# Row-wise max-norm of a float32 matrix: partial maxima folded in by VectorE's own last instruction of a row instead of by GpSimd

## The chip, the cores and the metric

The kernel runs on one core of a Trainium2 chip. The metric is device microseconds of one execution; three runs of the kernel before gave 628.87, 628.88 and 628.91 us, median 628.88 us. Times in the profile are counted from the first instruction that the profiler saw.

## The reference

```python
def setup_inputs():
    return {"x": np.random.randn(8192, 8192).astype(np.float32)}

def reference(x):
    return np.linalg.norm(x, ord=np.inf, axis=1)
```

The vector infinity norm of each of 8192 rows is the largest absolute value in the row. Every one of the 268.4 MB of x has to be read once, and the output is 32 KB.

## The kernel before

**Two parts.** The first 8192 - 18*128 = 5888 rows (the big part) are read by 23 loads. A load brings two whole rows to each of the 128 partitions (16384 columns of float32 a partition, 8 MB). The last 2304 rows (the tail) give each partition 18 rows that follow each other in memory, so a partition's tail is one run of 18*8192 = 147456 columns. It is cut into 29 loads without regard to where rows end. I number the loads 0 to 22 (big) and 23 to 51 (tail); load 23 is again 16384 wide, and the widths then fall to 704.

**The planner.** `tail_loads` chooses the widths. It holds two straight lines, `LOAD` (1.1775 ns a column and 73 ns a load) and `REDUCE` (1.0417 ns a column and 60 ns an instruction), and walks back from the end so that each load lands just before VectorE has finished with the one before it. The last piece of the last row is 704 wide, and the last piece of row 16 (768 wide) is loaded just before it, out of order.

**Pieces and rows.** Where a load ends inside a row, the row comes in pieces. In the tail, rows 0, 1, 2 and 4 to 8 are whole. Rows 3 and 9 to 14 have two pieces each, row 15 has three, row 16 five, row 17 seven. A load can hold the end of one row and the beginning of the next; VectorE then runs one instruction for each.

**The ring.** All loads land in one SBUF tensor, `ring`, of 3*16384 columns a partition, with 2048 more behind it (`APART`) for the last load. `Pieces.room` hands out places in order and goes back to column 0 when a load does not fit in what is left. All widths are multiples of 64, so every load begins at a multiple of 64 columns (256 bytes).

**Queues and waits.** All loads are issued by SyncE (L92) in order. A load's landing is counted on one of five semaphores in turn, and load i may be issued only after VectorE's last instruction for load i-5; it also waits for whatever VectorE still has to read in the columns that it overwrites. VectorE runs one `tensor_reduce` (maximum of absolute values, L110) a piece, in order of the loads; the first of a load waits for the load's semaphore. Consecutive instructions overlap a little: an instruction that waits for nothing starts about 0.08 us before the one before it ends.

**Partial maxima.** For rows 3 and 9 to 16 each piece's maximum goes to a small tensor `parts`, and GpSimd takes the maximum of them into `res_tail` (L207), ten instructions in all. Row 17 is done differently: its partial maxima are written to `ring` just behind the place of its last piece (load 51, at column 49152), and the instruction for that piece reads six columns more and takes them in.

**The end.** Two one-element memsets on VectorE (L218) keep the last store's wait apart from the last reduction. ScalarE issues the store of the big part (L221) and of tail rows 0 to 15 (L225). SyncE first waits for GpSimd's result of row 16 (`seen`, L236), then for VectorE's memsets, and issues the store of rows 16 and 17 (L240); the program ends when that has landed and the engines have met at a barrier.

Of the kernel before, what the change touches and what calls it, by code (L numbers as in the profile page):

```python
# [7 lines left out]
P = 128  # L8
R = 2
RING = 3 * 16384  # L10
APART = 2048
# [6 lines left out]
ROWS = 18  # L18
# [7 lines left out]
def tail_loads(n_cols, big):  # L26

    slack = 0.0
    lag = REDUCE[0] * FIRST + REDUCE[1]
    loads = []
    end = ROWS * n_cols

    def take(top, bottom, most):
        nonlocal slack  # L40
        w = 0
        n = 0
        spare = SPARE if loads else 0
        while True:

            n += 1
            start = max(bottom, (top - 1) // n_cols * n_cols - (n - 1) * n_cols)
            fit = int((lag + slack - spare - REDUCE[1] * n) / REDUCE[0])
            w = max(w, min(fit, top - start) // GRAIN * GRAIN)
            if fit <= top - start or start <= bottom:  # L50
                break
        w = max(GRAIN, min(w, most, top - bottom))
        row = (top - w + n_cols - 1) // n_cols * n_cols
        if top - row >= SNAP * w or (w == most and top > row):
            w = top - row
        n = (top - 1) // n_cols - (top - w) // n_cols + 1
        slack += (LOAD[0] - REDUCE[0]) * w + LOAD[1] - REDUCE[1] * n
        loads.append((top - w, w))
        return top - w

    ends = [take(end, end - n_cols, FIRST), take(end - n_cols, end - 2 * n_cols, n_cols)]
    for top, bottom in zip(ends, (end - n_cols, 0)):
        while top > bottom:
            top = take(top, bottom, big)
    return loads[::-1]
# [60 lines left out]
@with_exitstack  # L126
def kernel(
    ctx: ExitStack,
    tc: tile.TileContext,
    x: bass.AP,  # L130
    out: bass.AP,
):
    nc = tc.nc
    f32 = mybir.dt.float32
    n_rows, n_cols = x.shape

    tail = tail_loads(n_cols, R * n_cols)
    split = n_rows - ROWS * P
    n_big = split // (R * P)

    x_big = x[:split].rearrange("(p t r) m -> t p (r m)", p=P, r=R)
    x_tail = x[split:].rearrange("(p r) m -> p (r m)", p=P)

    single = ctx.enter_context(tc.tile_pool(name="single", bufs=1))
    ring = single.tile([P, RING + APART], f32)
    res_big = single.tile([P, n_big, R], f32)
    res_tail = single.tile([P, ROWS], f32)
    idle = single.tile([1, IDLE], f32)  # L150
    pieces = Pieces(tc, ring)

    for t in range(n_big):
        at = pieces.room(R * n_cols)
        pieces.load(at, R * n_cols, x_big[t])
        buf = ring[:, at : at + R * n_cols]
        pieces.reduce([(res_big[:, t, :], buf.rearrange("p (r m) -> p r m", r=R))])


    parts = []  # L160
    for i, (start, w) in enumerate(tail):
        c = 0
        while c < w:
            row = (start + c) // n_cols
            n = min(w - c, (row + 1) * n_cols - start - c)
            parts.append((row, i, c, n))
            c += n
    of_row = [[q for q in parts if q[0] == row] for row in range(ROWS)]

    spots, behind, dst = {}, {}, {}
    at = RING
    for row, own in enumerate(of_row):
        if row == ROWS - 1:
            spots[own[-1][1]] = at
            at += own[-1][3]
            for q in own[:-1]:
                dst[q] = ring[:, at : at + 1]
                at += 1  # L180
            behind[own[-1]] = len(own) - 1
            dst[own[-1]] = res_tail[:, row : row + 1]
        elif len(own) == 1:
            dst[own[0]] = res_tail[:, row : row + 1]
        else:
            some = single.tile([P, len(own)], f32, name=f"parts{row}")
            for k, q in enumerate(own):
                dst[q] = some[:, k : k + 1]
    assert at <= RING + APART and len(behind) == 1
    for i, (start, w) in enumerate(tail):  # L190
        at = spots[i] if i in spots else pieces.room(w)
        pieces.load(at, w, x_tail[:, start : start + w])
        done = pieces.reduce(
            [
                (dst[q], ring[:, at + q[2] : at + q[2] + q[3] + behind.get(q, 0)])
                for q in parts
                if q[1] == i
            ]
        )
        for row in range(ROWS - 1):  # L200
            if len(of_row[row]) > 1 and of_row[row][-1][1] == i:
                best = dst[of_row[row][0]]
                more = [dst[q] for q in of_row[row][1:]]
                while more:
                    two, more = more[:2], more[2:]
                    to = best if more else res_tail[:, row : row + 1]
                    combined = nc.gpsimd.tensor_scalar(  # L207
                        out=to,
                        in0=best,
                        scalar1=two[0],  # L210
                        scalar2=two[1] if len(two) == 2 else None,
                        op0=mybir.AluOpType.max,
                        **(dict(op1=mybir.AluOpType.max) if len(two) == 2 else {}),
                    )
                    tc.add_to_no_dep_group("combined", combined.ins)
    tc.declare_fence(done.ins, group="loads")
    for i in range(IDLE):
        rest = nc.vector.memset(idle[:, i : i + 1], 0.0)  # L218
        tc.keep_in_program_order(rest)

    early = nc.scalar.dma_start(  # L221
        out=out[:split].rearrange("(p q) -> p q", p=P), in_=res_big.rearrange("p t r -> p (t r)")
    )
    out_tail = out[split:].rearrange("(p r) -> p r", p=P)
    middle = nc.scalar.dma_start(  # L225
        out=out_tail[:, : ROWS - 2], in_=res_tail[:, : ROWS - 2]
    )
    for store in (early, middle):
        tc.add_manual_dep(
            store.ins,  # L230
            pieces.last[-3].name,
            mybir.DependencyInfo(mybir.DependencyClass.Sync, mybir.DependencyReason.DATA),
            reason="not beside the last load",
        )

    seen = nc.sync.keepalive_nop([nc.sync.lower_ap(res_tail[:, ROWS - 2 : ROWS - 1])])  # L236
    tc.keep_in_program_order(seen)
    tc.no_tile_sem_insts.add(seen.ins.name)
    tc.add_to_no_dep_group("seen", seen.ins)
    last = nc.sync.dma_start(out=out_tail[:, ROWS - 2 :], in_=res_tail[:, ROWS - 2 :])  # L240
    tc.declare_no_dep(last.ins, group="combined", reason="SyncE has waited for GpSimd")
    tc.declare_fence(last.ins, group="seen")
    for before in (rest, early, middle):
        gone = nc.sync.keepalive_nop([])
        tc.keep_in_program_order(gone)
        tc.add_manual_dep(
            gone.ins,
            before.ins.name,
            mybir.DependencyInfo(mybir.DependencyClass.Sync, mybir.DependencyReason.DATA),
            reason="done before the last store lands",  # L250
        )
# [28 lines left out]
```

## Time and profile before

| | before |
|---|---|
| median of three runs | 628.88 us |
| the profiled execution itself | 628.88 us |
| its span, first to last instruction | 627.1 us |
| outside the span | 1.78 us |
| VectorE busy | 552.1 us, 62 instructions |
| GpSimd busy | 3.2 us, 14 instructions |
| HBM read | 268.44 MB, 428 GB/s over the span |
| VectorE's wait for loads, big part | 69.4 us |
| VectorE's wait for loads, tail | 2.1 + 1.2 us |
| last store issued, span | 624.92 us |

A group line of the page reads: line, engine, operation, what is written from what, shapes, count, busy microseconds, mean nanoseconds of one, idle time of the engine just before, and what ended that idle time. Only gaps over 0.15 us count as idle there. DMA's own work stands in the lines on GB/s and in the time from a load's issue to its landing.

### The profile page before, as it was taken

Reading aid. Unit: us, or ns where it says so; the run is one execution under the profiler, and the core shown is the slowest. Engines: PE = TensorE matmul, PEld = TensorE weight load, DVE = VectorE, ACT = ScalarE, POOL = GpSimd, SP = SyncE. Lnnn points to the kernel's source line nnn. Section 1 sums busy time; section 2 is a strip of 40 time slices with the busy share of each in tenths; the row PEclk is TensorE's granted clock in tenths of the full one; section 3 lists DMA queues with packets and bytes.
Section 4 is the critical chain, followed back from the end, with each engine's and each line's share of the span. In section 5 each row is a group of like instructions: output and inputs, shape, how many; then the busy total and the mean of one; then the engine's idle time right before and its main releaser. Section 6 shows DMA issues by size and latency. Waiting matters only on the chain.

```text
span 627.1 us, 175 instructions
## 1 busy us (share of the span) xinstructions
DVE 552.1 (88%) x62; POOL 3.2 (1%) x14
## 2 busy tenths in 40 slices
DVE  0588988889988889888898888988889999999998
POOL 0000000000000000000000000000000000000000
DMA  9999999999999999999999999999999999999997
GB/s 401 410 460 401 468 401 468 401 468 401 468 401 468 401 468 401 468 401 468 401 464 405 451 418 451 418 439 431 422 437 442 404 435 442 430 422 430 426 422 308
DMA packets 7921, 268.48 MB, mean 428 GB/s; under 512 B 1264, under 2 KB 1264, under 8 KB 2416
## 3 DMA queue, kind: packets, MB, share of 16 engines
q1 hardware_dynamic: 7632, 268.44, 99.3%
q10 hardware_dynamic: 288, 0.03, 0.0%
q14 instruction: 1, 0.01, 0.0%
HBM read 268.44 MB, written 0.03 MB: 428 GB/s over the span
## 4 chain that ended last, share of the span: by engine, by line
DMA 57%; DVE 42%; issue 0%; DVEq 0%; SPq 0%
DMA ring<-in_x_dram 57%; DVE res_big L110 22%; DVE parts L110 12%; DVE res_tail L110 7%; DVE ring L110 1%; DVEq L275 0%; SPq L92 0%; DVE idle L218 0%
## 5 line engine op out<-in xcount | busy, mean ns | idle before, releaser
L110 DVE TENSOR_REDUCE res_big<-ring 128x2 f32<-128x16384 f32 x23 | 396.1, 17220 | 69.4 <-DMA ring<-in_x_dram 69.4
L110 DVE TENSOR_REDUCE parts<-ring 128x1 f32<-128x3136 f32 (+18 forms) x22 | 78.5, 3634 | 1.2 <-DMA ring<-in_x_dram 1.2
L110 DVE TENSOR_REDUCE res_tail<-ring 128x1 f32<-128x8192 f32 (+1 forms) x9 | 69.8, 7811 | 2.1 <-DMA ring<-in_x_dram 2.1
L110 DVE TENSOR_REDUCE ring<-ring 128x1 f32<-128x1600 f32 (+5 forms) x6 | 8.3, 1445 | 0.0
L207 POOL TENSOR_SCALAR res_tail<-parts 128x1 f32<-128x1 f32 x9 | 2.7, 296 | 615.6 <-DVE parts L110 615.6
L207 POOL TENSOR_SCALAR parts<-parts 128x1 f32<-128x1 f32 x1 | 0.4, 353 | 5.6 <-DVE parts L110 5.6
L264 POOL MEMSET const-bfloat16-1.0<- 128x1 bf16 x1 | 0.1, 101 | 0.0
L264 POOL MEMSET const-uint8-127<- 128x1 uint8 x1 | 0.1, 101 | 0.0
L264 POOL MEMSET const-float32-0.0<- 128x1 f32 x1 | 0.1, 99 | 0.2 <-issue 0.2
L264 POOL MEMSET const-float32-1.0<- 128x1 f32 x1 | 0.1, 98 | 0.0
L218 DVE MEMSET idle<- 1x1 f32 x2 | 0.1, 59 | 0.0
## 6 DMA issues: line engine op xcount, KB each, us to landing
ring<-in_x_dram SPq DMA_DIRECT2D x3, 4096.0 KB, 40.5
ring<-in_x_dram SPq DMA_DIRECT2D x1, 7264.0 KB, 31.1
ring<-in_x_dram SPq DMA_DIRECT2D x1, 5024.0 KB, 33.3
ring<-in_x_dram SPq DMA_DIRECT2D x1, 4544.0 KB, 34.6
ring<-in_x_dram SPq DMA_DIRECT2D x1, 4224.0 KB, 40.3
ring<-in_x_dram SPq DMA_DIRECT2D x1, 4032.0 KB, 35.5
ring<-in_x_dram SPq DMA_DIRECT2D x1, 3584.0 KB, 35.4
ring<-in_x_dram SPq DMA_DIRECT2D x2, 1568.0 KB, 18.3
```

What stands on the lines that cost most here:

```text
L110: ins = self.nc.vector.tensor_reduce(out=dst, in_=src, axis=mybir.AxisListType.X, op=mybir.AluOpType.max, apply_absolute_value=True,)
L207: combined = nc.gpsimd.tensor_scalar(out=to, in0=best, scalar1=two[0], scalar2=two[1] if len(two) == 2 else None, op0=mybir.AluOpType.max, ...
L218: rest = nc.vector.memset(idle[:, i : i + 1], 0.0)
L264: nc = _bacc.Bacc("TRN2", target_bir_lowering=False, num_devices=1)
```

## The change

GpSimd takes no part any more. For every tail row that comes in several pieces, the maxima of the pieces before the last are written to the columns of `ring` right in front of the place of the row's last piece, and VectorE's instruction for that last piece starts that many columns earlier. To make the room, `room` is asked for the piece's width plus the number of partial maxima, and the load starts behind them. Row 17's partials move from behind its last piece to the front of it, too. Where a load holds the end of a row and the beginning of the next, the beginning of the next row is now reduced first.

```diff
-    spots, behind, dst = {}, {}, {}
-    at = RING
+    ahead = [0] * len(tail)
+    for own in of_row:
+        assert own[-1][2] == 0 or len(own) == 1
+        ahead[own[-1][1]] += len(own) - 1
+    places = [pieces.room(ahead[i] + w) + ahead[i] for i, (_, w) in enumerate(tail[:-1])]
+    places.append(RING + ahead[-1])
+    dst = {}
     for row, own in enumerate(of_row):
...
+        at = places[own[-1][1]] - (len(own) - 1)
+        for k, q in enumerate(own[:-1]):
+            dst[q] = ring[:, at + k : at + k + 1]
+        dst[own[-1]] = res_tail[:, row : row + 1]
     for i, (start, w) in enumerate(tail):
-        at = spots[i] if i in spots else pieces.room(w)
+        at = places[i]
         pieces.load(at, w, x_tail[:, start : start + w])
...
-                while more:
-                    two, more = more[:2], more[2:]
-                    to = best if more else res_tail[:, row : row + 1]
-                    combined = nc.gpsimd.tensor_scalar(
...
+        mine = sorted((q for q in parts if q[1] == i), key=lambda q: -q[2])
+        pairs = []
+        for q in mine:
+            before = len(of_row[q[0]]) - 1 if q == of_row[q[0]][-1] else 0
+            pairs.append((dst[q], ring[:, at + q[2] - before : at + q[2] + q[3]]))
+        done = pieces.reduce(pairs)
...
-    seen = nc.sync.keepalive_nop([nc.sync.lower_ap(res_tail[:, ROWS - 2 : ROWS - 1])])
-    tc.keep_in_program_order(seen)
...
     last = nc.sync.dma_start(out=out_tail[:, ROWS - 2 :], in_=res_tail[:, ROWS - 2 :])
```

What follows from it for places, worked out from the widths: a load's width plus its partials is no longer a multiple of 64, so loads 25 to 27 and 30 to 51 begin 1 to 6 columns (4 to 24 bytes) past a multiple of 64 columns, load 50 nine columns past it. Load 28 no longer fits behind load 27 (8191 columns are left, 8192 are needed) and goes to column 0, where load 24 lay; load 34 goes back to column 1. VectorE has the same 60 reductions over the same columns.

More of the change, by code (lines that the diff above doesn't have):

```diff
@@ L168 @@
     of_row = [[q for q in parts if q[0] == row] for row in range(ROWS)]
-    spots, behind, dst = {}, {}, {}
-    at = RING
-    for row, own in enumerate(of_row):
[L175 to L188, printed above, removed]
@@ L189 @@
-    assert at <= RING + APART and len(behind) == 1
+    ahead = [0] * len(tail)
[4 more added lines that the diff above has]
+    places.append(RING + ahead[-1])
+    assert places[-1] + tail[-1][1] <= RING + APART
+    dst = {}
+    for row, own in enumerate(of_row):
+        at = places[own[-1][1]] - (len(own) - 1)
+        for k, q in enumerate(own[:-1]):
+            dst[q] = ring[:, at + k : at + k + 1]
+        dst[own[-1]] = res_tail[:, row : row + 1]
@@ L190 @@
     for i, (start, w) in enumerate(tail):
-        at = spots[i] if i in spots else pieces.room(w)
+        at = places[i]
         pieces.load(at, w, x_tail[:, start : start + w])
[L193 to L203, printed above, removed]
-                while more:
-                    two, more = more[:2], more[2:]
-                    to = best if more else res_tail[:, row : row + 1]
[L207 to L215, printed above, removed]
@@ L234 @@
         )
-    seen = nc.sync.keepalive_nop([nc.sync.lower_ap(res_tail[:, ROWS - 2 : ROWS - 1])])
-    tc.keep_in_program_order(seen)
-    tc.no_tile_sem_insts.add(seen.ins.name)
-    tc.add_to_no_dep_group("seen", seen.ins)
     last = nc.sync.dma_start(out=out_tail[:, ROWS - 2 :], in_=res_tail[:, ROWS - 2 :])
-    tc.declare_no_dep(last.ins, group="combined", reason="SyncE has waited for GpSimd")
-    tc.declare_fence(last.ins, group="seen")
     for before in (rest, early, middle):
```

## The prediction

> **What bounds the kernel now.** I read the busy shares and the DMA lines of the page first, then the table of stretches, then the chain of waits, then the last two microseconds instruction by instruction.
>
> ```profile
> span 627.1 us, 175 instructions
> DVE 552.1 (88%) x62; POOL 3.2 (1%) x14
> ...
> HBM read 268.44 MB, written 0.03 MB: 428 GB/s over the span
> ...
> L110 DVE TENSOR_REDUCE res_big<-ring 128x2 f32<-128x16384 f32 x23 | 396.1, 17220 | 69.4 <-DMA ring<-in_x_dram 69.4
> ...
> L207 POOL TENSOR_SCALAR res_tail<-parts 128x1 f32<-128x1 f32 x9 | 2.7, 296 | 615.6 <-DVE parts L110 615.6
> ```
>
> VectorE is 88% busy, but in the big part it waits 69.4 us for loads: there the transfer is the bound. GpSimd's ten combining instructions take 3.1 us in all. The table of stretches (columns: length, VectorE busy and instructions, GpSimd busy, clock, share of the DMA engines, GB/s):
>
> ```profile
> 41.80:467.60 425.80, 378.83 (x22) 0.00 (x0) 1.00 1.00 432
> ...
> 497.00:546.00 49.00, 49.00 (x6) 0.28 (x1) 1.00 1.01 434
> 546.00:594.00 48.00, 48.00 (x12) 1.39 (x5) 1.00 0.99 426
> 594.00:624.00 30.00, 30.00 (x16) 0.99 (x3) 1.00 0.98 404
> ```
>
> From 497 us on both are full: VectorE 49.00 of 49.00, 48.00 of 48.00, 30.00 of 30.00 us, and the DMA engines 0.98 to 1.01. The chain of waits names VectorE for this stretch, but only by a hair. A load's landing is its issue plus its time to landing. By that, load 30 landed at 546.61 and VectorE began it at 546.65; load 37: 594.00 and 594.05; load 46: 618.28 and 618.30; load 51: 623.95 and 624.01. A reduction that really waits for a load starts 0.023 us after the landing (467.596 to 467.619), so the two are within 0.04 us of each other from 546 us to the end. Whatever slows either of them in the tail moves the end; making one faster gains nothing beyond 0.04 us.
>
> ```profile
> 623.15 0.94 DVE L110 TENSOR_REDUCE parts<-ring 128x1 f32<-128x768 f32 x1
> ...
> 624.01 0.89 DVE L110 TENSOR_REDUCE res_tail<-ring 128x1 f32<-128x710 f32 x1
> 624.27 0.36 POOL L207 TENSOR_SCALAR res_tail<-parts 128x1 f32<-128x1 f32 x1 [10.84 <-DVE parts L110]
> 624.84 0.06 DVE L218 MEMSET idle<- 1x1 f32 x2
> 624.92 0.35 SPq L240 DMA_DIRECT2D out_dram<-res_tail  x1
> ```
>
> In these rows (start, length) GpSimd's last instruction ends at 624.63 and VectorE's memsets at 624.90; the last store is issued 0.025 us after the memsets. GpSimd is 0.27 us off the path.
>
> **The change part by part.**
>
> *GpSimd and SyncE's wait for it go: 0.* Ten instructions, 3.1 us, all beside VectorE and DMA. SyncE's wait for GpSimd ended at 624.67, before VectorE's end at 624.90, which stays and releases the store. ScalarE's store of rows 0 to 15 waited for a GpSimd instruction that ended at 607.5, and is still held behind the big store to 623.68.
>
> *Longer reads: +0.014 us.* 19 partial maxima are read in front of pieces, six of which row 17 read before; 13 more elements at 1.05 ns (8676 ns for 8192 less 4275 ns for 3968, over 4224 columns, is 1.04).
>
> *Order inside a load: 0.* Where a load holds an end and a beginning, the same two instructions run in the other order, with the same sum. The load's columns come free at the same end.
>
> *VectorE's waits on itself.* Twelve reductions more than before now wait for an earlier reduction: to read partials that it wrote, or to write partials where something was read before. Counting back in the order of the instructions, the awaited one is two or more places back in all but one case, so it ended before the waiting instruction could start. The last instruction of before has such a wait, two places back, and started at 624.008, 0.086 us before its predecessor's end at 624.094: no cost. The exception is row 14: load 37's reduction takes in what load 36's, directly ahead of it, wrote. Before, it started at 594.046, 0.081 us ahead of its predecessor's end. Now it must start behind it. The nearest rows: SyncE issues 0.028 us after a VectorE end (594.127 to 594.155), GpSimd with a wait of its own in front 0.177 us after (624.094 to 624.271). That gives 0.11 to 0.26 us of delay. The same extra wait on VectorE was over 0.060 us after the end it could have waited for (623.234 to 623.294), and a start after a landing takes 0.023; so I take 0.081 + 0.060 + 0.023 = 0.16. Queued behind it are all later reductions, and SyncE's issue of load 42, which has four loads in front of it and so time. VectorE has 0.008 us of slack at load 41 and 0.034 at load 46; so 0.12 us reach the end (0.07 to 0.22).
>
> *A rule on this.* The Trainium skill, "VectorE: DVE Perf Modes", section "The DRAIN you can't avoid", says that a semaphore after each VectorE instruction cost nothing over one after the last alone. By that rule the stall would be 0 and the end 0.12 us earlier than by my rows.
>
> *Loads that go elsewhere in the ring: 0.* With the first of load 23's halves reduced last and load 28 back at column 0, loads 26 to 31 are issued later. Load 26 goes out at the end of load 23's reduction, 484.9 instead of 465.9, 28 with load 24's at 495.5 instead of 484.9, 29 with 25's at 512.0 (was 495.5), 30 at 520.6 (512.1), 31 at 529.2 (520.6). The queue runs dry only if a load is issued after the one before it has landed; those landings are 496.7, 516.1, 525.8, 535.8 and 546.6. The shortest lead is 11.7 us, load 26's, and a load needs about 1 us from issue to its first packet. From load 33 on the rule of five semaphores decides, as before. If the cover were gone, each late microsecond would be one at the end.
>
> *Loads that begin off the 64-column grid: unknown.* 25 loads, 25 to 27 and 30 to 51, write each partition from 4 to 36 bytes past a multiple of 256 bytes. No transfer of the trace before does this at size. These loads take 623.95 - 479.49 less 19.73 for loads 28 and 29, so 124.7 us. From below: nothing (same bytes, same source; nothing in the trace suggests a gain). From above: if the engine writes in units and each unit now touches one slot of 32 bytes more. By landings, a load of 8192 columns took 9.71 us and one of 16384 took 19.35; so 0.07 us of a load is fixed, 9 ns for each of the 8 packets that an engine handles of it, and 32 bytes cost 1.18 ns (9.64 us/8 for 32768 bytes). One slot more a packet is 200 packets x 1.2 ns = 0.24 us; a second packet for each packet is 200 x 9 ns = 1.8 us; nine slots where there were eight, over all the bytes, is 124.7/8 = 15.6 us. I take one slot a packet, as in the trace's rows cost goes by bytes moved with a fixed part a packet, and keep 0 and 15.6 for the range.
>
> *A rule on this.* The skill's "DMA: Bandwidth & Descriptors", section "How a descriptor splits into AXI transactions", says that a descriptor that starts off a 256-byte boundary has its first transaction begin at the boundary below, and the unused bytes still cost. For 4 to 36 bytes at its 32-byte beats that is an estimate of one or two beats a packet, 0.24 to 0.5 us. The rule tells of reading; no run here shows the writing side.
>
> **Sum.** DMA and VectorE run side by side, so their delays don't add. VectorE's path: 0.12 + 0.01 = 0.13 us. DMA's: 0.24 less its slack of 0.04 = 0.20 us. The end moves by the larger, 0.20 us. The profiled execution took 628.88 us, its span 627.1 and 1.78 outside; the median of the runs is the same 628.88. Prediction: 628.88 + 0.2 = 629.1 us.
>
> **Rivals.**
>
> *Every unit written costs more (the other side).* If off-grid writes are cut so that something is paid all along a packet, the 25 loads slow down together. For it: the DMA engines are at 0.98 to 1.01 with nothing left to give. Against: the engine sees one long run, and could cut it at the grid after the first piece. Nine slots for eight gives 628.9 + 15.6 = 644.5 us; one more in sixteen, 7.8 us, gives 636.7. It decides from 1.0% of 124.7 us on (1.26 us, 0.2% of the time, about what a measurement of this kernel can tell from no change).
>
> *A fixed price a packet.* If each off-grid packet is handled as two, 1.8 us: 630.7 us, slower. Against it: the 9 ns is the price of a whole packet, and only its ends differ.
>
> *VectorE's waits cost each time.* If all twelve held up the pipeline as row 14's does, 12 x 0.16 = 1.9 us, 630.8 us. The last instruction of before speaks against it.
>
> *GpSimd's share was felt after all.* If GpSimd's instructions disturbed VectorE, their loss would be a gain. But the reductions that a GpSimd instruction ran beside are as long as the others (8.675 us for 8192 columns at 503.35 with one, 8.675 at 511.95 without), and DMA leaves 0.04 us. That gives 628.84 us, no measurable gain.
>
> **How the numbers follow.** Forecast, no price beyond ends of packets and one stall: 0.46, with a range of its own of 628.8 to 629.5. Off-grid writing that costs all along: 0.28. A price a packet of 6.3 ns or more: 0.14. VectorE's waits: 0.08. Faster, by something that no row shows: 0.04. Slower is 0.28 + 0.14 + 0.08 = 0.50, same 0.46, faster 0.04. The range goes from 628.8 to 645, the dearer price of writing; what is left out above it and below is about 0.12.
>
> **What would show it.** Right: the reduction of 128x4224 (load 36) followed after about 0.08 us by that of 128x3969, the others overlapping; the stretch before the end at 426 to 434 GB/s; load 51 landing at about 624.1; no L207, last store issued at about 625.1. Wrong: VectorE's idle time in the tail ended by loads, GB/s lower from load 25 on while load 28 and 29, which are on the grid, keep their rate (the writing rival); small gaps before every reduction that waits for itself; a gap in the DMA line near 497 or 512 us.

## The result and the profile after

The changed kernel takes 629.60 us (median of 22 runs, 629.33 to 630.11) against 628.87 us (22 runs, 628.74 to 629.16): a ratio of 1.0012, 95% interval 1.0006 to 1.0017. So it is slower by 0.73 us, 0.12%. That is less than the 0.2% that the prediction took for the smallest change that can be told, but it is clear of noise: no run of the changed kernel is as short as the longest of the kernel before. It lies inside the range given (628.8 to 645 us) and 0.1 us above the range of the likeliest case (628.8 to 629.5). The sum had 0.2 us, and most of the loss comes from something that it did not contain.

The page of the changed kernel:

```profile
span 627.9 us, 168 instructions
...
DVE 552.3 (88%) x62; POOL 0.2 (0%) x4
...
L110 DVE TENSOR_REDUCE res_tail<-ring 128x1 f32<-128x8192 f32 (+10 forms) x18 | 115.5, 6454 | 3.4 <-DMA ring<-in_x_dram 3.3
L110 DVE TENSOR_REDUCE ring<-ring 128x1 f32<-128x3136 f32 (+14 forms) x19 | 42.0, 2255 | 0.6 <-DMA ring<-in_x_dram 0.6
```

VectorE is busy 0.2 us longer than before (552.3 against 552.1 us), no more. What is new stands at the end of the last line: the 3.3 us of the line above are the two waits of 2.1 and 1.2 us that were there before, but the 0.6 us among the instructions that write to the ring are a wait for a load late in the tail. VectorE's instructions in order of time, from 594 us on, show where, and the table of stretches (length, VectorE busy and count, GpSimd, clock, share of the DMA engines, GB/s), first before, then after, shows it beside DMA:

```profile
589.52 4.55 DVE L110 TENSOR_REDUCE ring<-ring 128x1 f32<-128x4224 f32 x1
594.17 4.29 DVE L110 TENSOR_REDUCE res_tail<-ring 128x1 f32<-128x3969 f32 x1
598.37 3.41 DVE L110 TENSOR_REDUCE ring<-ring 128x1 f32<-128x3136 f32 x1
602.38 4.35 DVE L110 TENSOR_REDUCE ring<-ring 128x1 f32<-128x3136 f32 x2 [0.60 <-DMA ring<-in_x_dram]
```

```profile
594.00:598.00 4.00, 4.00 (x2) 0.00 (x0) 1.00 1.01 427
598.00:606.00 8.00, 8.00 (x4) 0.28 (x1) 1.00 1.00 423
```

```profile
594.00:598.00 4.00, 3.90 (x2) 0.00 (x0) 1.00 1.01 427
598.00:606.00 8.00, 7.40 (x4) 0.00 (x0) 1.00 1.01 422
```

Row 14's stall is the missing 0.1 us between 594 and 598 us (4.55 us after 589.52 the first instruction ends, and the second starts 0.10 us later). The 0.60 us at 602.38 is a wait for load 39, and the load is late, not VectorE early: load 38 took 19.5 us from issue to landing before and 19.4 after, load 39, issued next, 17.2 and 18.1. The two answers on DMA issues, load 39 before and after:

```profile
ring<-in_x_dram SPq DMA_DIRECT2D x1, 1568.0 KB, 17.2
```

```profile
ring<-in_x_dram SPq DMA_DIRECT2D x1, 1568.0 KB, 18.1
```

By issue plus time to landing, load 38 lands 130.11 us after load 23 (130.18 before), load 39 then 4.72 us later (3.77 before), and every load from there to the last keeps that lag: load 51 lands at 624.74 (623.95). So 0.95 us were lost between two neighbouring loads, at one time. In the DMA view of 597.5 to 599 us of the changed kernel stands what the same stretch of before does not have:

```profile
q1 hardware_dynamic: 51, 0.64, 103.3%
q14 instruction: 1, 0.01, 1.4%
```

One packet of 8192 bytes on the queue called "instruction", by that name a piece of some engine's program. By the packet records it ran from 598.09 for 0.33 us; the load packet that started as it ended, at 598.41 (12544 bytes), took 1.13 us where the others take 0.47. The records do not name the DMA engine; that the two shared one is read from these times, and in all eight kernels of this document that have this packet among the loads the load packet that starts there is longer in the same way. Together that is 0.33 + 0.66 = 0.99 us on one of sixteen engines, and a load has landed when its slowest engine is done. Before, the same packet comes at 624.45 us, behind the last load, among the stores:

```profile
q10 hardware_dynamic: 288, 0.03, 11.0%
q1 hardware_dynamic: 27, 0.05, 6.1%
q14 instruction: 1, 0.01, 1.5%
```

(That is before, 623 to 625 us.) The changed kernel's end, in order of time:

```profile
624.82 0.88 DVE L110 TENSOR_REDUCE res_tail<-ring 128x1 f32<-128x710 f32 x1
625.64 0.06 DVE L195 MEMSET idle<- 1x1 f32 x2
625.73 0.35 SPq L213 DMA_DIRECT2D out_dram<-res_tail  x1
```

The last store is issued 0.81 us later than before and the span is 0.8 us longer; nothing behind the last load has changed its length.

### The profile page after: what moved, and what is told of

Same layout as the page of the kernel before. It is cut to its first block, busy times and chain, and to the rows that moved or that the text cites. A ratio compares the mean times of both kernels' runs of the same rounds, so it can differ in the third digit from the quotient of the medians.

```text
span 627.9 us, 168 instructions
## 1 busy us (share of the span) xinstructions
DVE 552.3 (88%) x62; POOL 0.2 (0%) x4
## 4 chain that ended last, share of the span: by engine, by line
DMA 60%; DVE 37%; issue 2%; DVEq 0%; SPq 0%
DMA ring<-in_x_dram 60%; DVE res_big L110 22%; DVE res_tail L110 10%; DVE ring L110 5%; DVEq L246 0%; SPq L92 0%; DVE idle L195 0%
## 5 line engine op out<-in xcount | busy, mean ns | idle before, releaser
L110 DVE TENSOR_REDUCE res_tail<-ring 128x1 f32<-128x8192 f32 (+10 forms) x18 | 115.5, 6454 | 3.4 <-DMA ring<-in_x_dram 3.3
L110 DVE TENSOR_REDUCE ring<-ring 128x1 f32<-128x3136 f32 (+14 forms) x19 | 42.0, 2255 | 0.6 <-DMA ring<-in_x_dram 0.6
```

Of the source, the lines that this page charges most:

```text
L110: ins = self.nc.vector.tensor_reduce(out=dst, in_=src, axis=mybir.AxisListType.X, op=mybir.AluOpType.max, apply_absolute_value=True,)
```

## The experiments

An instruction of VectorE that has to wait for a load and for an earlier reduction gets a second instruction in front of it that does nothing but wait; I call it a stand-alone wait. The trace counts them, one before and eight after:

```profile
L110 DVEq EVENT_SEMAPHORE  x1: 21/21/21, 623.3 to 623.3; - x1
```

```profile
L110 DVEq EVENT_SEMAPHORE  x8: 21/21/21, 467.6 to 624.1; - x8
```

Theory A: the time is lost to the packet on the instruction queue, which VectorE's program, longer by seven stand-alone waits, brings forward into the loads. Theory B: loads off the 64-column grid. Theory C: VectorE's waits on itself. Theory D: GpSimd's program, or its absence. All runs below are compared with the kernel before on the same chip.

**Seven memsets more in the kernel before.**

```diff
         pieces.reduce([(res_big[:, t, :], buf.rearrange("p (r m) -> p r m", r=R))])
+        if t < 7:
+            more = nc.vector.memset(extra[:, t : t + 1], 0.0)
+            tc.keep_in_program_order(more)
```

> The kernel before with seven one-element memsets on VectorE, one behind each of the first seven reductions of the big part, where VectorE waits 2.1 us for every load (7 x 0.06 us, hidden). Seven is by how many waits of its own VectorE's program is longer in the changed kernel. Theory A (the changed kernel loses its time to one 8 KB packet on the instruction queue, which VectorE's longer program brings forward from behind the last load, 624.4 us, to 598.1 us, and which holds up one DMA engine): the 8 KB packet is seen at 590 to 605 us, one load after it lands about 0.8 us later than before, and the time is 0.7 to 0.8 us longer, 629.6 us, although nothing of the change is in it. Theory B (loads off the 64-column grid) and theory C (VectorE's waits on itself): all loads are on the grid and no wait is added, so 628.9 us. Theory D (the fetch belongs to GpSimd's program or to the mere absence of GpSimd): GpSimd is as before, so 628.9 us.

Measured: 629.52 us, ratio 1.0011 (1.0002 to 1.0019). The kernel before, with nothing of the change in it, loses 0.66 us to seven memsets that cost VectorE 0.4 us inside a wait 400 us earlier. The packet is seen, at 560.07 us and so earlier than expected, and the load that it hits is late. DMA view of 560 to 562.5 us, and VectorE's order of time:

```profile
q14 instruction: 1, 0.01, 0.8%
```

```profile
555.07 9.86 DVE L110 TENSOR_REDUCE parts<-ring 128x1 f32<-128x1152 f32 x3
565.78 13.54 DVE L110 TENSOR_REDUCE parts<-ring 128x1 f32<-128x7168 f32 x2 [0.86 <-DMA ring<-in_x_dram]
```

The price is not VectorE's; it is a wait for a load. B, C and D don't explain it.

**Two memsets, and one.** The same edit with `t < 2` and with `t < 1`.

> The same with two memsets. Theory A: two instructions more bring the 8 KB packet forward by about two reductions, from 624.4 to about 621 to 623 us, in the last loads; as they are still under way, most of the 0.8 us is paid: 629.2 to 629.7 us. If it still comes behind the last packet of the loads (623.5 us), 628.9. Theories B, C and D: 628.9 us.

> The kernel before with one one-element memset more on VectorE, behind the first reduction of the big part. Theory A (the 8 KB packet on the instruction queue comes among the loads once VectorE's program is longer than some length): two more instructions brought it from 624.4 to 587.8 us. If before lies right at that length, one is enough: packet near 590 to 595 us, 629.5 us; if not, the packet stays behind the loads and the time at 628.9 us. Theories B (loads off the grid) and C (VectorE's waits): 628.9 us.

Measured: with two 629.53 us, 1.0011 (1.0002 to 1.0020), packet at 587.79; with one 628.84 us, 1.0001 (0.9992 to 1.0010), packet at 624.35. So the forecast for two was right on the time and wrong on the place: a second instruction moves the packet by 36.6 us, from behind the loads to the middle of the tail. It is a threshold, not a shift by two reductions.

**The loads back on the grid.**

```diff
-    places = [pieces.room(ahead[i] + w) + ahead[i] for i, (_, w) in enumerate(tail[:-1])]
-    places.append(RING + ahead[-1])
+    whole = [-(-n // GRAIN) * GRAIN for n in ahead]
+    places = [pieces.room(whole[i] + w) + whole[i] for i, (_, w) in enumerate(tail[:-1])]
+    places.append(RING + whole[-1])
```

> The changed kernel with the room in front of a piece rounded up to 64 columns, so that all loads begin on the grid again; VectorE's instructions, their waits and GpSimd's absence are as in the changed kernel. Theory A: the 8 KB packet is where it was, 598 us, and the time stays 629.6 us. Theory B: back to 628.9 us. Theory C: 629.6 us.

Measured: 629.49 us, 1.0011 (1.0002 to 1.0020), packet at 598.47. Theory B falls: the loss stays with all loads on the grid. The changed kernel's own trace says the same from the other side. Loads 24 to 38, twelve of them off the grid, land 130.11 us after load 23 where it was 130.18 before; so those twelve paid no more than their aligned selves. Three other traces with all of these loads on the grid (this one, before with one memset, and before with two memsets and a holding wait, below) have 130.11, so the figure moves by 0.07 us without any cause named here. A price of even one slot of 32 bytes a packet, 12 x 8 x 1.2 ns = 0.12 us, should have shown beside that.

**GpSimd's program as long as before.**

```diff
     pieces = Pieces(tc, ring)
+    extra = single.tile([1, 12], f32)
+    for i in range(12):
+        more = nc.gpsimd.memset(extra[:, i : i + 1], 0.0)
+        tc.keep_in_program_order(more)
```

> The changed kernel with twelve one-element memsets on GpSimd at the start, so that GpSimd's program is as long as before. Theory A (it is VectorE's program that counts): the 8 KB packet stays at 598 us, 629.6 us. Theory D (the packet is GpSimd's, or moves with GpSimd's length): the packet goes back behind the loads and the time to 628.9 us. Theories B and C: 629.6 us.

Measured: 629.59 us, 1.0013 (1.0004 to 1.0022), packet at 598.25. Theory D falls.

**VectorE's program cut back to the length of before**, in two forms, with and without the two memsets at the end. A wait is dropped where the load that the instruction waits for was itself issued only after the awaited reduction.

```diff
+ORDERED = {24: tuple(range(0, 22, 3)), 29: (25,), 30: (26,), 50: (40, 41, 42, 43)}
...
+            if not k:
+                for j in ORDERED.get(i, ()):
+                    self.tc.declare_no_dep(
+                        ins.ins, group=f"load{j}", reason="this load was issued behind it"
+                    )
...
+        if len(mine) == 2 and all(q[3] == n_cols for q in mine):
+            two = ring[:, at : at + 2 * n_cols].rearrange("p (r m) -> p r m", r=2)
+            pairs = [(res_tail[:, mine[1][0] : mine[0][0] + 1], two)]
```

> The changed kernel with VectorE's program cut back to the length of before: four waits of VectorE on itself dropped that the issue of the load in question has already waited for, the two whole rows of load 23 reduced by one instruction, and the two memsets at the end left out (the last store waits for the last reduction itself). GpSimd stays away, the loads stay off the grid, row 14's stall stays. Theory A: the packet is back behind the loads and the time at 628.9 to 629.1 us, what is left over 628.9 being row 14's stall of 0.19 us less VectorE's slack. Theory B: 629.6 us. Theory C: at least half of the loss stays, as the stall and half of the waits do: 629.3 us or more.

> The same with the two memsets at the end kept, so VectorE's program is two instructions longer than that of before. The two stand behind the last reduction, where they cost nothing by themselves. Theory A: as with two memsets more in the kernel before, the packet is among the loads (585 to 595 us) and the time 629.5 us. Theories B and C: the same as with the memsets left out.

Measured: without the memsets 629.45 us, 1.0010 (1.0001 to 1.0019), packet at 598.36; with them 629.57 us, 1.0011 (1.0002 to 1.0020), packet at 598.29. Here theory A as I had put it failed: the program is as long as that of before, and the packet is where the changed kernel has it. It is not the length that counts.

What does, can be read from where the stand-alone waits stand, counted from VectorE's first reduction. The sequencer is the part of an engine that takes in its program and hands the work on; a stand-alone wait is handled by it alone. In before there is one, the 60th; with one memset more it is the 61st, with two the 62nd. In the changed kernel they are the 26th, 34th, 37th, 42nd, 47th, 50th, 65th and 67th; in the cut-back one the 38th, 43rd, 46th and 62nd. Theory A2: VectorE's sequencer runs ahead of the reductions and stops only at such a wait; when it comes to about the 62nd instruction, it asks for the next 8 KB. In before, and with one memset, a wait in the 60th or 61st place holds it until 623.2 or 623.3 us, and the packet follows 1.13 to 1.15 us later. In the changed kernel the last wait before the 62nd place is row 14's, the 50th; it is passed at 594.13, and the packet comes at 598.09. In the cut-back one it is the 46th, for the same row, passed at 594.20, packet at 598.36. The same place in time, whatever the length.

**Sixteen memsets more in the changed kernel.** The edit of the first experiment with `t < 16`, in the changed kernel.

> The changed kernel with 16 one-element memsets on VectorE, one behind each of the first 16 reductions of the big part. Theory A: the packet moves forward by some 16 reductions, to about 480 to 530 us. As the DMA engines are full all along, the engine that is held up has no time to catch up: the price stays, 629.5 to 629.8 us. If the time instead falls back towards 628.9, an engine can catch up over the loads behind it. Theories B and C: 629.6 us.

Measured: 629.70 us, 1.0014 (1.0005 to 1.0023). The packet is at 561.74 us, not at 480 to 530: now row 11's wait is the 58th and the next the 63rd; row 11's is passed at 557.60, and the packet follows 4.1 us later. That fits A2 and not a shift by sixteen. The price was paid in full 36 us earlier than in the changed kernel, and with seven memsets in before 64 us ahead of the end: the engine that is held up does not catch up, as all of them are full.

**One wait more, in the right place.** Two kernels that lose the time, the cut-back one with its memsets (629.57) and before with two memsets (629.53), each with one addition:

```diff
                 ins.wait_op(self.sems[i % SEMS], 16 * (i // SEMS + 1), "sem-ge")
+                if i == 50:
+                    self.tc.add_manual_dep(
+                        ins.ins,
+                        self.last[48].name,
...
+                        reason="VectorE's sequencer stops here",
+                    )
```

> The cut-back changed kernel with the memsets at the end (629.6 us), and one wait more on VectorE: ahead of load 50's reduction it also waits for load 48's, two places back, which stands in the program as an instruction of its own, the 61st from the first reduction. Theory A2 (the packet is asked for when VectorE's sequencer, which runs some 16 instructions ahead of the reductions and stops only at such waits, comes to about its 62nd instruction; in before the wait ahead of the last reduction is the 60th and stops it there): the sequencer is held until 622.2 us, the packet comes at 623.4 us or later, behind the loads, and the time is 628.9 to 629.1 us although a wait was added. If it comes between 622.2 and 623.4 it hits the last packets: up to 629.5. Theory A (length of VectorE's program): still too long by three, packet at 598 us, 629.6 us. Theory C (VectorE's waits cost): 629.6 us or more.

> The kernel before with two memsets more (629.5 us), and the same wait ahead of load 50's reduction, the 61st instruction. Theory A2: packet behind the loads again, 628.9 us. Theory A: 629.5 us, as the program is longer still. Theory C: 629.5 us or more.

Measured: 629.04 us, 1.0004 (0.9995 to 1.0012), packet at 623.61; and 628.90 us, 1.0002 (0.9993 to 1.0011), packet at 623.30. Adding an instruction to a program that was too long took away 0.5 and 0.6 us; in neither pair does a run of the one kernel reach into the runs of the other (629.42 to 629.91 against 628.84 to 629.30, and 629.39 to 629.91 against 628.76 to 629.26). A2 stands, A as the length does not, and neither does C. The traces do not show the sequencer's place itself; A2 is inferred from where the packet comes, and these two kernels are its test. DMA view of 623 to 625 us and the order of time of the cut-back kernel with the holding wait:

```profile
q1 hardware_dynamic: 32, 0.05, 7.2%
q14 instruction: 1, 0.01, 1.5%
```

```profile
589.63 4.54 DVE L112 TENSOR_REDUCE ring<-ring 128x1 f32<-128x4224 f32 x1
594.28 4.29 DVE L112 TENSOR_REDUCE res_tail<-ring 128x1 f32<-128x3969 f32 x1
598.48 7.66 DVE L112 TENSOR_REDUCE ring<-ring 128x1 f32<-128x3136 f32 x3
```

```profile
623.33 1.74 DVE L112 TENSOR_REDUCE res_tail<-ring 128x1 f32<-128x772 f32 x2
...
625.01 0.06 DVE L217 MEMSET idle<- 1x1 f32 x2
625.10 0.35 SPq L235 DMA_DIRECT2D out_dram<-res_tail  x1
```

The wait of 0.60 us for load 39 is gone. Its load 51 lands at 623.95 as before, all 25 loads still off the grid, and VectorE has no gap but row 14's; yet its last memsets end at 625.08, 0.18 us later than before, or 0.14 us when both are counted from the landing of load 23. With the packet out of the way, row 14's stall comes through. That rests on the trace: the median, 0.23 us above that of before, is not clear of noise by its interval.

**Row 14 alone by GpSimd again**, in that kernel.

```diff
+    two14 = single.tile([P, 2], f32)
+    for k, q in enumerate(of_row[14]):
+        dst[q] = two14[:, k : k + 1]
...
+        if of_row[14][-1][1] == i:
+            nc.gpsimd.tensor_scalar(
+                out=res_tail[:, 14:15], in0=two14[:, 0:1], scalar1=two14[:, 1:2],
...
```

> The cut-back changed kernel with the holding wait (629.04 us, VectorE's last instructions 0.18 us later than before), and row 14 alone combined as before: its two partial maxima go to a small tensor and one GpSimd instruction takes the larger, so load 37's reduction waits for nothing that VectorE has just written. All else stays: 25 loads off the grid, the other rows folded in by VectorE. If row 14's stall is what is left: load 37's reduction starts 0.08 us before its predecessor's end again, VectorE's memsets end within 0.05 us of before's 624.90 (counted from the same landing of load 23), 628.85 us. If off-grid loads or longer reads are what is left: 629.0 us.

Measured: 629.00 us, 1.0002 (0.9993 to 1.0011). Neither forecast is met cleanly. The stall is gone (load 37's reduction starts 0.09 us before its predecessor's end), and VectorE is in step with before up to load 50. But the packet, at 623.69, now comes between the last load's data (the last packet ends at 623.45) and its landing: load 51 lands 1.05 us after load 50 where it was 0.85, and VectorE begins it 0.08 us after it has run dry. So the end is again 0.2 us late, it seems for another reason; that the packet held up the landing is read from the order of time and was not tried. That the stall alone makes up the last 0.2 us rests on the trace of the run before this one.

No version found is faster than the kernel before, and the traces say why none was to be had by relieving VectorE alone: load 51 lands within 0.06 us of VectorE's start on it there.

| kernel | us | packet at us |
|---|---|---|
| before | 628.81 to 628.87 | 624.45 |
| before, 1 memset | 628.84 | 624.35 |
| before, 2 memsets | 629.53 | 587.79 |
| before, 2 memsets and holding wait | 628.90 | 623.30 |
| before, 7 memsets | 629.52 | 560.07 |
| changed | 629.60 | 598.09 |
| changed, loads on the grid | 629.49 | 598.47 |
| changed, 12 GpSimd memsets | 629.59 | 598.25 |
| changed, 16 memsets | 629.70 | 561.74 |
| changed, cut back | 629.45 | 598.36 |
| changed, cut back, memsets at the end | 629.57 | 598.29 |
| the same with holding wait | 629.04 | 623.61 |
| the same, row 14 by GpSimd | 629.00 | 623.69 |

With the packet among the loads the kernels are 0.60 to 0.85 us slower than before on their chip; with it behind them, within 0.23 us.

## Why the prediction was right or wrong

*What bounds the kernel.* Right, and it is what makes the case: DMA and VectorE are within 0.04 us of each other from 546 us on, so 0.95 us lost on one DMA engine cost 0.8 us at the end.

*GpSimd and SyncE's wait for it, 0.* Right: the last store is issued 0.02 us after the memsets, as before, and a GpSimd program of the old length changed nothing.

*VectorE's waits on itself.* The count was right, 12 more with only row 14's on the instruction directly ahead. That stall was sized at 0.16 us and measured 0.18: the reduction starts at 594.169, 0.103 us after its predecessor's end, instead of 0.081 us ahead of one; I had 0.083 for the 0.103. In the changed kernel it reaches the end only in part or not at all, since VectorE then waits 0.6 us for load 39; where the packet was held back, VectorE's end moved 0.14 us, counted from the landing of load 23, against the 0.12 forecast. The rule quoted from the Trainium skill ("VectorE: DVE Perf Modes", "The DRAIN you can't avoid"), that a semaphore between VectorE instructions costs nothing, measured there on `tensor_copy`, does not hold for this one: 0.18 us.

*The failed step.* It is this same step where it counted a wait's own delay as its whole cost and priced the other eleven waits at "no cost". Their time on VectorE is indeed nothing: those instructions overlap as before. But seven of the twelve, row 14's among them, are instructions of their own in VectorE's program. I looked at each wait's own delay and not at the program's places, and no part of the sum asked when the next piece of the program is fetched, though the page of before has the line for it (the "instruction" queue, one packet). The added waits move the place of every later instruction, and the last stop ahead of the 62nd place became row 14's; that took the fetch from 624.45 to 598.09 us, where it made a load 0.95 us late. The rival "VectorE's waits cost each time" named the right instructions with the wrong mechanism: 1.9 us of stalls did not happen.

*Loads off the grid, 0.24 us taken, 0 to 15.6 kept.* Measured nothing: no lag by load 38, no lag at load 51 where the packet was held back, and no gain clear of noise from putting them back on the grid (629.49 against 629.60 us). The term that carried the sum was therefore zero, and the two cases of dear off-grid writing, 0.42 of the 0.50 given to slower, had nothing behind them. The estimate from the skill's "DMA: Bandwidth & Descriptors" (0.24 to 0.5 us) is not borne out on the writing side either.

*Loads issued later, 0.* Right: loads 26 and 28 to 31 were issued when forecast (484.9, 495.4, 512.0, 520.6, 529.2) and landed as before.

*Order in a load, longer reads, 0 and 0.014 us.* Right within what the trace can tell: VectorE's busy time is 0.2 us longer in all.

So the likeliest case, no change to speak of, came true to 0.12%, but not by its reasons. Its 629.1 us was reached by two terms, one of which is zero and the other mostly hidden; 0.73 us is three and a half times the 0.2 us of the sum, and 629.60 us lies just above that case's own range. That the time is inside the whole range is luck: the room above was kept for off-grid writing, which cost nothing, and no case held the loss that came.

## What to carry to other kernels

Where all DMA engines are full to the end, as here, anything else that they carry can move the end, the program's own fetching too (0.60 to 0.85 us here): look for the packet on the instruction queue, see whether it falls among the loads, and compare its place before and after an edit. A wait that is always met cost its engine no time here, but a stand-alone one is an instruction, and where it stands decided how far the sequencer ran ahead; counting instructions and stand-alone waits belongs to the pricing of any edit that adds dependencies. When a loss appears between two neighbouring transfers and then stays, look for one event at that time, not for a rate.

## What the runs showed of the hardware that was not expected

One fetch of 8192 bytes took 0.33 us on its engine and stretched the load's packet behind it by 0.66 us (12544 bytes: 1.13 instead of 0.47 us; 16896 bytes, in before with two memsets: 1.29 instead of 0.63; 28672 bytes at 560 us: 1.73 instead of 1.07), the same for all three sizes. The Trainium skill ("Runtime: NRT & Kernel Launch", "Instruction fetch mechanics") says that an engine refills its program in 16 KiB blocks through a DMA queue of its own and calls the cost mostly hidden; here the one packet of the execution has 8192 bytes, and beside saturated loads the cost was 0.60 to 0.85 us.

The fetch was asked for when VectorE's sequencer could come to its 62nd instruction from the first reduction: a stand-alone wait in the 60th or 61st place holds it back, one in the 62nd doesn't. From the passing of the last wait to the packet it took 4.0 to 4.2 us among the loads (594.13 to 598.09, 594.20 to 598.36, 557.60 to 561.74), whether 12, 16 or 4 places lay between, and 1.1 to 1.5 us at the end (623.29 to 624.45, 622.48 to 623.61, 622.23 to 623.69). What fills the 4 us was not tried. Where no wait stops the sequencer (2 and 7 memsets in before), taking off those 4 us leaves it 18 or 19 places ahead of the running reduction; that lead is an estimate from two runs. A stand-alone wait whose condition has long been met is still passed only in its turn: in the changed kernel the one in the 34th place waits for load 25's reduction, which ended at 511.97, and it was passed at 525.80, 0.06 us after the landing (525.74) of load 28, whose reduction stands in front of it.

Starting a float32 load 4 to 36 bytes off a 256-byte boundary in SBUF changed no landing by more than the 0.07 us by which landings differ from trace to trace (15 loads, 130.11 us; with the packet held back, load 51 156.31 us after load 23 where before had 156.35).
